# Which weight sums a transfer adds up, and when turned parts are copied out, in the MLP of a hybrid decoder block

## The chip, the core and the metric

The kernel runs on one core of a Trainium2 chip. Times are device microseconds for one execution. Its engines work side by side, each through its own list of instructions in order: PE (TensorE) multiplies, DVE (VectorE) and ACT (ScalarE) work on tiles elementwise, POOL (GpSimd) and SP (SyncE) here mostly issue transfers (DMAs). Engines wait for each other through semaphores.

## What is computed

One decoder layer for 256 tokens of width 2048 in float32: attention and a gated convolution, merged and added to the residual; an MLP; a gated per-layer embedding. The change lies in the MLP, the second line below:

```python
r = r + merged @ w_o[i]
h = rms_norm(r, g_mlp[i])
r = r + jnp.square(jax.nn.relu(h @ w_up[i])) @ w_down[i]   # w_up 2048 x 8192, w_down 8192 x 2048
h = rms_norm(r, g_ple[i])
r = r + jax.nn.sigmoid(h @ w_ple_gate[i]) * (p[i] @ w_ple_proj[i])
```

## The kernel before

**Splitting.** A float32 factor is multiplied as a high and a low part: ACT rounds the tile to `hi` (line 87, `w_hi`, `b_hi`, `t_hi`), DVE forms `lo` = tile − `hi` (line 101, `w_lo`, `b_lo`, `t_lo`), and PE (line 90) multiplies three of the four combinations.

**Units.** The MLP goes through 72 units `g`: 64 `up` units, each 128 columns of `w_up`, and 8 `dn` units, each 128 columns of the last quarter of `w_down`. PE does a unit's columns (`cols`, 32 matmuls into `ps_up` or `ps_dn`), then a piece of the product with the rest of `w_down`.

**Items.** That product uses a scheme of seven products per block of two by two, `P1` to `P7`, accumulated in seven PSUM banks over a run of items. An *item* (side, j) is one such block of weights; there are 56, numbered here from 0 in the order of `items`. Runs with one side follow each other: items 0 to 3, then five runs of eight (4 to 11, 12 to 19, ... 36 to 43), and a last one of twelve (44 to 55). Items 48 to 55 are *halved*: unit g = 55 makes the first half (0, 1) of item 48 and unit 56 the second half (2, 3), and so on to unit 70. The scheme needs sums of weight blocks. `load_pair` loads four blocks into `raw_s` (SP, 256 KB each), and `make` splits `B11` and `B22` (`b_hi`, `b_lo`), forms the sums for `T1`, `T3` (called `t13`) and later those for `T2`, `T4`, and splits these too (`t_hi`, `t_lo`). PE multiplies an item one unit after it was made.

**`ADDED`** (line 684) says for which items the two sums of `t13` are made by a transfer: `load_added` loads the third block twice into a tile `t` one unit ahead (SP), `load_pair` leaves that block out, and an accumulating DMA on POOL (line 702) adds two blocks of `raw_s` into `t`. For the other items DVE adds (`raw_s<-raw_s` 128x1024).

**Ends of runs.** At the end of a run the seven banks are copied by ACT (`part`) and added to DRAM by seven accumulating DMAs on POOL (`store`, line 825, `part_P<-part`). These are put into the list `filling`; `fill()` emits one at chosen places of the next unit's work.

**Parts into outputs.** Late in the MLP `fetch_part` loads the finished products (`part_in`, SP) for one side and half; `jobs` combine them (ACT scales, DVE `part_in<-part_in,scales`), up to four each time `run_jobs` is called, which only halved items do. Two results of each fetch are `turned`: `turn_part` transposes one on PE (line 863) into a bank of PSUM, ACT copies it out (`part_out`) and POOL adds it to the residual kept in DRAM (line 868, `r_kept`). The bank is the one that the next unit's columns write, so these wait for `part_out`. The transposes stand on PE between the first and the second piece of products of a halved unit. The copy goes through `filling` as well: in `make` it is emitted by a `fill()` behind the `high` of a sum.

The order of instructions on each engine is that of the code: every matmul, activation, DVE operation and SP load keeps its program order (`inorder`, `load`), and POOL's DMAs go out one after the other.

Of the kernel before, what the change touches and what calls it, by code (L numbers as in the profile page):

```python
# [38 lines left out]
def hybrid_block_kernel(ctx: ExitStack, tc: tile.TileContext, ins: dict, out: bass.AP):  # L39
# [571 lines left out]
    N_GROUP, GROUP = 6, 4  # L611
# [7 lines left out]
    NU = len(units)  # L619
# [4 lines left out]
    items = []  # L624
# [47 lines left out]
    def half_tiles(name):  # L672
        return tuple(wp.tile([P, HALF], F32R, tag=t, name=f"{name}_{t}") for t in ("hi", "lo"))
# [7 lines left out]
        wU[g].append((hi, lo))  # L681
        return lambda: high(hi, raw), lambda: low(lo, raw, hi)

    ADDED = set(items[4::2])

    def pair_part(a, n, d):
        side, j = a
# [16 lines left out]
    def load_added(a):  # L704

        wS[a] = {}
        if a in ADDED:
            t = wS[a]["t13"] = wp.tile([P, 2, CW], F32, tag="t", name="t13", bufs=2)
# [25 lines left out]
    def make(a, xs, evacuate, work):  # L734


        w, j = wS[a], a[1]
        raw = w["raw"]
        flat, halves = "p a f -> p (a f)", "p (a f) -> p a f"
        fresh = None  # L740
        if 0 in xs:
            if j not in sums:
                fresh = sum_u(j)
                sums[j] = tuple(slot([P, 4, P], F32R, f"s_{i}") for i in range(2))
            sh, sl = sums[j]
            for i in range(4):
                w[f"S{i + 1}"] = sh[:, i, :], sl[:, i, :]
            hi, lo = half_tiles("b")
            keep(w, ("B11", "B22"), hi, lo)
            src = raw[:, 0:2, :].rearrange(flat)  # L750
            high(hi, src)
            evacuate()
            if fresh is not None:
                high(sh, fresh)
            low(lo, src, hi)
            if a in ADDED:
                t13 = w["t13"]
            else:
                t13 = raw[:, 0:3:2, :]
                dve.tensor_add(t13, raw[:, 0:2, :], raw[:, 2:3, :].to_broadcast([P, 2, CW]))  # L760
            w["raw13"] = t13
        if 2 in xs:
            b21 = w["B21"] = tuple(slot([P, CW], F32R, f"b21_{n}") for n in range(2))
            high(b21[0], raw[:, 3, :])
            evacuate()
            fill()
            dve.tensor_add(raw[:, 1, :], raw[:, 1, :], w["raw13"][:, 0, :])
            if 0 in xs:
                low(b21[1], raw[:, 3, :], b21[0])
                dve.tensor_add(raw[:, 3, :], raw[:, 1, :], raw[:, 3, :])  # L770
                raw24 = raw[:, 1:4:2, :]
            else:
                dve.tensor_add(raw[:, 2, :], raw[:, 1, :], raw[:, 3, :])
                low(b21[1], raw[:, 3, :], b21[0])
                raw24 = raw[:, 1:3, :]
                work()
        if 0 in xs:
            if fresh is not None:
                low(sl, fresh, sh)
            if 2 not in xs:  # L780
                work()
            t13 = half_tiles("t13")
            keep(w, ("T1", "T3"), *t13)
            view = [t.rearrange(halves, a=2) for t in t13]
            high(view[0], w["raw13"])
            fill()
            low(view[1], w["raw13"], view[0])
        if 2 in xs:
            t24 = half_tiles("t24")
            keep(w, ("T2", "T4"), *t24)  # L790
            view = [t.rearrange(halves, a=2) for t in t24]
            high(view[0], raw24)
            fill()
            low(view[1], raw24, view[0])
# [36 lines left out]
    jobs, turns_due = [], []  # L831
# [27 lines left out]
    def turn_part(u, src):  # L859
        ps = bank("ps_part").rearrange("p (i s) -> p i s", i=2)  # L860
        for i in range(2):
            for t in range(NT):
                inorder(nc.tensor.transpose(ps[:, i, t * P:(t + 1) * P], src[t][:, i * P:(i + 1) * P], ident))

        def out():
            st = slot([P, 2, S], F32, "part_out")
            act(st, ps, AF.Copy)
            nc.gpsimd.dma_start(r_kept[u], st, accum_op=ALU.add)

        filling.append(out)  # L870

    filling = []

    def fill(n=1):
        for _ in range(min(n, len(filling))):
            filling.pop(0)()
# [61 lines left out]
        r[u] = slot([P, 2, S], F32, f"r_{u}")  # L938
        nc.gpsimd.dma_start(r[u], r_kept[u])

    fetching = {NU - 18: (1, 0), NU - 16: (1, 1), NU - 14: (0, 0), NU - 12: (0, 1)}

    for g in range(2):
        load_raw(g)
# [6 lines left out]
    for g in range(NU):  # L951
        kind, i = units[g]
        ordered[0] = g > 1
        if g in (5, 7):
            banks["acc"] = [7, 5] if g == 5 else [7]
        reach = 1 if FIRST <= g < NU - 8 else 2
        for n in range(g + 2, g + reach + 2):
            load_raw(n)
        for a, x in staged[g + 1]:
            if x == 0:  # L960
                load_pair(a)
        for a, x in staged[g + 2]:
            if x == 0:
                load_added(a)
        if g in fetching:
            fetch_part(*fetching[g])
        for u in {NU - 8: (4, 5, 6, 7), NU - 4: (0, 1), NU - 3: (2, 3)}.get(g, ()):
            load_r(u)
        if g == NU - 3:
            ss2 = slot([P, 2, S], F32, "ss2")  # L970
        if g == NU - 2:
            praw = slot([P, 2, S], F32, "p")
            load(praw, ins["pT"].rearrange("p (k s) -> p k s", s=S))
        xs = hT if kind == "up" else {k: uT[16 * i[0] + k] for k in range(16)}
        ps = cols(wU[g][1:], xs, f"{kind}_{g}")
        ending = any(a in last_of for a, _ in staged[g - 1])
        carried = len(filling)
        if ending:
            assert not filling
            for a, x in staged[g - 1]:  # L980
                products(a, x)
        if g == 0:
            rstd1 = rstd_columns(ss1, "mlp", 1)
            scales = const.tile([P, 2 * NT], F32, name="scales")
            dve.tensor_mul(scales[:, :NT], rstd1, rstd1)
            dve.tensor_scalar_mul(scales[:, NT:], scales[:, :NT], -1.0)
            up0, up1, down0, down1 = (scales[:, t:t + 1] for t in range(2 * NT))
        if g == 1:
            row1 = rstd_rows(rstd_diag(scales, "mlp"), "mlp")
        done = [n for n in range(g) if n in evac] if g > 1 else []  # L990
        ups = [units[n][1] for n in done if units[n][0] == "up"]
        for k in ups:
            up_sum(k, evac.pop(done.pop(0)))
        halves = []
        while made < g + reach:
            made += 1
            load_raw(made)
            halves += [(made, 0), (made, 1)]
        for h in halves:
            on_act, on_dve = unit_half(*h)  # L1000
            on_act()
            fill()
            on_dve()
        for k in ups:
            up_high(k)
        for k in ups:
            up_low(k)
        for n in done:
            dn_done(*units[n][1], evac.pop(n))
        taken = []  # L1010

        queue = [] if ending else list(staged[g - 1])

        def take():
            if taken:
                return
            taken.append(evacuated(ps, kind))
            if ending:
                side = staged[g - 1][0][0][0]
                filling.extend(lambda name=name: store(side, name) for name in NAMES)  # L1020
            if due and queue:
                products(*queue.pop(0))
                turn_part(*due.pop(0))

        due = [turns_due.pop(0)] if turns_due else []

        def run_jobs():
            for _ in range(min(4, len(jobs))):
                jobs.pop(0)()

        fill(carried)
        if staged[g]:
            make(staged[g][0][0], [x for _, x in staged[g]], take, run_jobs)
        take()
        if g == NU - 1:
            p1 = [evacuated(prod["P1"], "p1", by) for by in (up0, up1)]
            d, e = (slot([P, CW], F32, n) for n in "de")
            scaled(d, prod["P5"], up0, p1[0], ALU.subtract)
            scaled(e, prod["P3"], up0, d)
        entering = {NU - 2: (8, 9), NU - 1: (10, 11, 12, 13, 14)}.get(g, ())  # L1040
        for n in entering:
            enter_high(n)
            if n % 2 == 1:
                square(n // 2)
        for n in entering:
            enter_low(n)
        evac[g] = taken[0]
        if kind == "up" and i == 63:
            up_sum(i, evac.pop(g))
            up_high(i)  # L1050
            up_low(i)
        for a, x in queue:
            products(a, x)
        assert not due
# [188 lines left out]
```

## Time and profile before

| | us |
|---|---|
| median of 3 runs (lowest to highest) | 1442.47 (1440.68 to 1443.04) |
| the profiled execution | 1441.09 |
| its span | 1439.3 |
| PE busy in it | 1417.1 |

By stage, from the windows of the profile (length; busy time of PE, PEld, DVE, ACT and POOL with instructions; PE's clock as a share of full speed; mean DMA share; GB/s):

```profile
0.00:631.00 631.00, 629.52 (x2907) 523.29 (x2908) 404.93 (x680) 333.77 (x617) 139.93 (x230) 1.00 0.71 231
631.00:860.00 229.00, 229.00 (x1206) 197.42 (x1205) 201.67 (x282) 164.30 (x247) 15.87 (x24) 1.00 0.77 235
860.00:1170.00 310.00, 304.02 (x1541) 257.74 (x1541) 275.80 (x366) 224.15 (x328) 35.83 (x42) 0.99 0.91 255
1170.00:1284.00 114.00, 105.56 (x549) 88.58 (x548) 104.58 (x162) 80.17 (x122) 14.16 (x18) 0.97 0.93 269
1284.00:1334.00 50.00, 47.52 (x250) 40.19 (x250) 41.15 (x63) 27.75 (x39) 3.96 (x6) 0.99 0.70 216
1334.00:1439.30 105.30, 101.48 (x598) 89.77 (x596) 80.13 (x139) 55.49 (x95) 1.64 (x1) 0.99 0.41 145
```

All before the MLP lies ahead of 631 us. The MLP goes to about 1327; behind it come the gate of the embedding and the output. In every stage PE is busy for most of the time; where its busy time is short of the window, it waits. In rows of the timeline, `1.02 <-ACT up` in brackets at the end of a row says that the engine was idle for 1.02 us before it, and that ACT's instruction that wrote `up` ended that. Equal instructions that follow each other closely make one row (x2).

### The profile page before, as it was taken

The numbers are of one execution on the slowest core, as the hardware profiler recorded it, in microseconds if no ns is written. First come the engines' busy times: TensorE is split into PE (matmuls) and PEld (weight loads), VectorE is DVE, ScalarE is ACT, GpSimd is POOL, SyncE is SP. The second block draws the span as 40 slices with busy tenths as digits, with TensorE's granted clock in tenths as the row PEclk, the third lists the DMA queues.
The fourth block names the chain that finished last, engine by engine and source line by source line (L and its number), as shares of the span: only waits on it lengthen the run. The fifth ranks groups of instructions, "written<-read, shape, count | busy, mean of one in ns | idle before, by whom it ended". The sixth has DMA issues, their size and how long they took to land.

```text
span 1439.3 us, 19925 instructions
## 1 busy us (share of the span) xinstructions
PE 1417.1 (98%) x7041; PEld 1197.0 (83%) x7041; DVE 1108.2 (77%) x1688; ACT 885.6 (62%) x1446; POOL 211.4 (15%) x321
## 2 busy tenths in 40 slices
PE   9999999999999999999999999999999999989998
PEld 7888888888888888888888888887887877878888
DVE  7676666766565647757999989898979989978984
ACT  6765545554544544546777868676767867665752
POOL 0043464302020200000000101001010100110000
PEclk9999999999999999999999999999999999999999
DMA  9868787766666675645797978989898899996470
GB/s 279 307 224 250 228 248 238 234 208 208 209 207 204 215 256 205 212 165 172 222 299 237 312 232 240 267 238 274 246 254 248 243 296 264 262 276 208 144 259 23
DMA packets 224052, 335.07 MB, mean 233 GB/s; under 512 B 13904, under 2 KB 148304, under 8 KB 209872
## 3 DMA queue, kind: packets, MB, share of 16 engines
q1 hardware_dynamic: 204000, 287.61, 61.1%
q0 software_dynamic: 19808, 46.16, 14.2%
q8 instruction: 55, 0.90, 0.2%
q14 instruction: 45, 0.37, 0.1%
q10 hardware_dynamic: 144, 0.04, 0.0%
HBM read 294.95 MB, written 24.64 MB: 222 GB/s over the span
## 4 chain that ended last, share of the span: by engine, by line
PE 81%; DVE 8%; DMA 6%; issue 3%; ACT 2%; SPq 0%; DVEq 0%; POOLq 0%; ACTq 0%
PE ps_up L90 16%; PE ps_g L90 12%; PE P L90 11%; PE ps_o L90 7%; PE ps_pg L90 6%; PE ps_y L90 6%; DMA raw_s<-in_w_down_dram 4%; PE ps_q L90 3%; PE ps_k L90 3%; PE ps_cx L90 3%; PE ps_cb L90 3%; PE ps_cc L90 3%; PE ps_v L90 3%; PE ps_dn L90 3%; DMA t<-raw_s 2%
## 5 line engine op out<-in xcount | busy, mean ns | idle before, releaser
L101 DVE TENSOR_TENSOR w_lo<-raw,w_hi 128x512 fp32r<-128x512 f32 (+1 forms) x524 | 468.2, 927 | 186.6 <-ACT w_hi L87 161.0
L87 ACT ACTIVATE w_hi<-raw 128x512 fp32r<-128x512 f32 (+1 forms) x524 | 406.9, 816 | 259.3 <-PE ps_g L90 63.3
L90 PE MATMUL ps_up<-x,w_hi 128*128 128x512 f32 x1024 | 255.8, 393 | 6.5 <-ACT part_out L87 3.5
L90 PEld LDWEIGHTS ps_up<-x,w_hi 128*128 128x128 f32 x1024 | 192.4, 189 | 47.6 <-ACT up L87 5.9
L90 PE MATMUL ps_g<-w_hi,x 128*128 128x512 f32 x512 | 158.2, 389 | 0.0
L87 ACT ACTIVATE t_hi<-raw_s 128x1024 fp32r<-128x1024 f32 x86 | 91.2, 1061 | 84.7 <-DVE raw_s L101 84.7
L90 PEld LDWEIGHTS ps_up<-x,w_lo 128*128 128x128 f32 x1024 | 131.3, 191 | 5.0
L90 PE MATMUL ps_up<-x,w_lo 128*128 128x256 f32 x1024 | 132.8, 283 | 0.0
L90 PE MATMUL P<-t_hi,s 128*128 128x512 f32 x336 | 123.4, 394 | 0.3 <-ACT t_hi L87 0.3
L101 DVE TENSOR_TENSOR t_lo<-raw_s,t_hi 128x1024 fp32r<-128x1024 f32 x86 | 103.9, 1221 | 15.5 <-ACT t_hi L87 15.5
L90 PEld LDWEIGHTS ps_g<-w_hi,x 128*128 128x128 f32 x512 | 96.1, 188 | 19.9
L90 PE MATMUL ps_g<-w_lo,x 128*128 128x512 f32 x256 | 99.6, 389 | 0.0
L101 DVE TENSOR_TENSOR raw_s<-raw_s 128x512 f32<-128x512 f32 (+1 forms) x116 | 96.2, 829 | 3.8
L702 POOL DMA_DIRECT2D t<-raw_s x26 | 22.2, 853 | 447.7 <-DMA raw_s<-in_w_down_dram 199.5
L90 PE MATMUL ps_y<-w_hi,x 128*128 128x512 f32 x256 | 79.4, 389 | 0.0
L90 PEld LDWEIGHTS P<-t_hi,s 128*128 128x128 f32 x336 | 63.6, 189 | 13.2 <-ACT t_hi L87 0.7
L101 DVE TENSOR_TENSOR b_lo<-raw_s,b_hi 128x1024 fp32r<-128x1024 f32 x56 | 68.3, 1219 | 3.4 <-ACT b_hi L87 3.4
L90 PE MATMUL P<-t_lo,s 128*128 128x512 f32 x168 | 66.1, 394 | 3.7 <-DVE t_lo L101 3.7
L90 PE MATMUL ps_pg<-x,w_hi 128*128 128x512 f32 (+1 forms) x272 | 69.1, 385 | 0.5 <-DVE x L101 0.5
L87 ACT ACTIVATE up<-ps_up 128x512 f32<-128x512 f32 x64 | 37.6, 588 | 37.2 <-PE ps_up L90 37.2
L87 ACT ACTIVATE a<-a 128x256 f32<-128x256 f32 x128 | 53.2, 415 | 11.6 <-DVE a L101 9.6
L87 ACT ACTIVATE b_hi<-raw_s 128x1024 fp32r<-128x1024 f32 x56 | 58.8, 1050 | 1.8 <-PE ps_dn L90 1.8
(238 smaller groups left out, 2583.2 us busy)
## 6 DMA issues: line engine op xcount, KB each, us to landing
raw<-in_w_up_dram SPq DMA_DIRECT2D x64, 1024.0 KB, 7.6
raw<-in_w_in_dram SPq DMA_DIRECT2D x56, 1024.0 KB, 5.4
raw_s<-in_w_down_dram SPq DMA_DIRECT2D x198, 256.0 KB, 4.4
raw<-in_w_branch_dram SPq DMA_DIRECT2D x16, 1024.0 KB, 5.7
raw<-in_w_o_dram SPq DMA_DIRECT2D x16, 1024.0 KB, 4.9
t<-in_w_down_dram SPq DMA_DIRECT2D x52, 256.0 KB, 5.3
t<-raw_s POOLq DMA_DIRECT2D x26, 512.0 KB, 7.9
raw_first<-in_w_qkv_dram SPq DMA_DIRECT2D x48, 256.0 KB, 6.6
```

What stands on the lines that cost most here:

```text
L87: return inorder(nc.scalar.activation(*args, **kw))
L90: return inorder(nc.tensor.matmul(*args, **kw))
L101: return lambda *args, **kw: inorder(getattr(nc.vector, name)(*args, **kw))
L702: nc.gpsimd.dma_start(wS[a]["t13"], raw[:, 0:2, :], accum_op=ALU.add)
```

## The change

Three edits:
- `ADDED` held every second item from 4 on: in each run of eight the first, third, fifth and seventh, and in the last run 44, 46, 48, 50, 52, 54. It now holds the first, fifth and seventh of each run (44 of the last run's first four), and all of items 48 to 55. So items 6, 14, 22, 30, 38, 46 are added by DVE, and 49, 51, 53, 55 by transfer: 24 transfers instead of 26, of which 8 instead of 4 fall in the last run's halved items.
- The copy of a turned part goes into a list of its own, `turned_out`. `out_turned()` empties it in the second half of an item right behind the evacuation of the columns, in the first half ahead of `high` of the sum, and again behind `take()`.
- The four fetches move from g = 54, 56, 58, 60 to 53, 56, 59, 62; `run_jobs` does up to three jobs instead of four; a turn is taken from its list only in a unit with products to put it between.

```diff
-    ADDED = set(items[4::2])
+    LAST = len(items) - 8
+    ADDED = {items[n] for n in range(GROUP, LAST) if (n - GROUP) % (2 * GROUP) in (0, 4, 6)} | set(items[LAST:])
...
             high(b21[0], raw[:, 3, :])
             evacuate()
+            out_turned()
             fill()
...
             if 2 not in xs:
                 work()
+            out_turned()
             t13 = half_tiles("t13")
...
-        filling.append(out)
-
-    filling = []
+        turned_out.append(out)
+
+    filling, turned_out = [], []
+
+    def out_turned():
+        while turned_out:
+            turned_out.pop(0)()
...
-    fetching = {NU - 18: (1, 0), NU - 16: (1, 1), NU - 14: (0, 0), NU - 12: (0, 1)}
+    fetching = {53: (1, 0), 56: (1, 1), 59: (0, 0), 62: (0, 1)}
...
-        due = [turns_due.pop(0)] if turns_due else []
+        due = [turns_due.pop(0)] if turns_due and queue else []
 
         def run_jobs():
-            for _ in range(min(4, len(jobs))):
+            for _ in range(min(3, len(jobs))):
...
         take()
+        out_turned()
```

**ACT in units 57 and 58 (item 49).** Before: `b_hi` to `w_hi` is unit 57, the rest unit 58. `up` is the evacuation of the unit's columns, `s` and `part_in` are other work of the unit, `t_hi` the high part of a sum.

```order
L87 ACTIVATE b_hi<-raw_s 128x1024
L87 ACTIVATE up<-ps_up_11212 128x512
L87 ACTIVATE s_11265<-s_raw 128x512
L87 ACTIVATE part_in<-part_in,scales 128x256 x2
L87 ACTIVATE t_hi<-raw_s 128x1024
L87 ACTIVATE part_out<-ps_part 128x512
L87 ACTIVATE w_hi<-raw 128x1024 x2
L87 ACTIVATE a<-a 128x256 x2
L87 ACTIVATE x<-a 128x256
L87 ACTIVATE b_0_11369<-raw_s 128x512
L87 ACTIVATE up<-ps_up_11321 128x512
L87 ACTIVATE part_out<-ps_part 128x512
```

After, the same place:

```order
L87 ACTIVATE b_hi<-raw_s 128x1024
L87 ACTIVATE up<-ps_up_11201 128x512
L87 ACTIVATE s_11254<-s_raw 128x512
L87 ACTIVATE t_hi<-t_11009 128x1024
L87 ACTIVATE w_hi<-raw 128x1024 x2
L87 ACTIVATE a<-a 128x256 x2
L87 ACTIVATE x<-a 128x256
L87 ACTIVATE b_0_11336<-raw_s 128x512
L87 ACTIVATE up<-ps_up_11288 128x512
L87 ACTIVATE part_out<-ps_part 128x512
L87 ACTIVATE part_in<-part_in,scales 128x256 x2
L87 ACTIVATE t_hi<-raw_s 128x1024
```

The first turned part leaves unit 57 and comes out in unit 58, directly behind `up`; the sum of item 49 comes from `t` (a transfer) instead of `raw_s` (a sum by DVE).

**SP at units 53 and 54.** `t` and `raw_s` are the blocks of an item, `raw` the weights of a unit, `part_in` the fetch. Before:

```order
L96 DMA raw_s<-in_w_down_dram 128x4x128 x4
L96 DMA t_10819<-in_w_down_dram 128x4x128 x2
L96 DMA raw<-in_w_up_dram 128x2048
L96 DMA raw_s<-in_w_down_dram 128x4x128 x3
L96 DMA part_in<-part_P_5554 128x256
L96 DMA part_in<-part_P_5556 128x256
```

After:

```order
L96 DMA raw_s<-in_w_down_dram 128x4x128 x4
L96 DMA t_10806<-in_w_down_dram 128x4x128 x2
L96 DMA part_in<-part_P_5554 128x256
L96 DMA part_in<-part_P_5556 128x256
L96 DMA part_in<-part_P_5551 128x256
L96 DMA part_in<-part_P_5552 128x256
L96 DMA part_in<-part_P_5550 128x256
L96 DMA part_in<-part_P_5553 128x256
L96 DMA part_in<-part_P_5555 128x256
L96 DMA raw<-in_w_up_dram 128x2048
L96 DMA raw_s<-in_w_down_dram 128x4x128 x3
```

The seven loads of the fetch now stand ahead of the weights of unit 56 and of the blocks of item 48.

**POOL at the start of the last run.** `part_P` are the stores of the run that has ended, `t` the sums of items, `r_kept` the turned parts. Before:

```order
L825 DMA part_P_5555<-part 128x512
L702 DMA t_10595<-raw_s 128x1024
L825 DMA part_P_5556<-part 128x512
L702 DMA t_10819<-raw_s 128x1024
L702 DMA t_11209<-raw_s 128x1024
L868 DMA r_kept_4718<-part_out 128x512
L868 DMA r_kept_4720<-part_out 128x512
```

After:

```order
L828 DMA part_P_5555<-part 128x512
L828 DMA part_P_5556<-part 128x512
L703 DMA t_10806<-raw_s 128x1024
L703 DMA t_11009<-raw_s 128x1024
L703 DMA t_11198<-raw_s 128x1024
L871 DMA r_kept_4718<-part_out 128x512
L871 DMA r_kept_4720<-part_out 128x512
```

The sum of item 46 (`t_10595`) between the last two stores is gone, and the sum of item 49 (`t_11009`) has come in between those of items 48 and 50.

## The prediction

> **What bounds the kernel now.** I read the page's first part, then the windows of the MLP, where all edits lie, then PE's timeline there, and behind each of its gaps the timeline of the engine that ended it.
>
> ```profile
> PE 1417.1 (98%) x7041; PEld 1197.0 (83%) x7041; DVE 1108.2 (77%) x1688; ACT 885.6 (62%) x1446; POOL 211.4 (15%) x321
> 860.00:1284.00 424.00, 409.58 (x2089) 346.32 (x2089) 380.38 (x527) 304.32 (x448) 49.99 (x60) 0.99 0.92 259
> ```
>
> TensorE is the bound: the change leaves every matmul in place, so it can only win what PE loses. The second line is the window from 860 to 1284 us (length; busy time of PE, PEld, DVE, ACT, POOL; clock, DMA share, GB/s). PE idles 424.00 − 409.58 = 14.42 us there. These are PE's gaps of over 0.2 us in it (start, duration, what waited, in brackets the idle time and what ended it):
>
> ```profile
> 913.77 0.39 PE L90 MATMUL P<-t_hi,x 128*128 128x512 f32 x1
> 914.00 0.39 PE L90 MATMUL P<-t_lo,x 128*128 128x512 f32 x1
> ...
> 915.61 0.73 PE L90 MATMUL ps_up<-x,w_hi 128*128 128x512 f32 x2 [0.99 <-ACT up L87]
> 996.30 0.50 PE L90 MATMUL P<-t_lo,s 128*128 128x512 f32 x1 [0.66 <-DVE t_lo L101]
> 1000.79 0.73 PE L90 MATMUL ps_up<-x,w_hi 128*128 128x512 f32 x2 [1.02 <-ACT up L87]
> 1080.90 0.50 PE L90 MATMUL P<-t_hi,s 128*128 128x512 f32 x1 [0.29 <-ACT t_hi L87]
> 1083.05 0.50 PE L90 MATMUL P<-t_lo,s 128*128 128x512 f32 x1 [1.65 <-DVE t_lo L101]
> 1169.20 0.50 PE L90 MATMUL P<-t_lo,s 128*128 128x512 f32 x1 [1.36 <-DVE t_lo L101]
> 1173.69 0.50 PE L90 MATMUL ps_up<-x,w_hi 128*128 128x512 f32 x1 [1.02 <-ACT up L87]
> ...
> 1203.54 3.66 PE L90 MATMUL ps_up<-x,w_hi 128*128 128x512 f32 x9 [2.70 <-ACT part_out L87]
> 1222.82 0.50 PE L90 MATMUL ps_up<-x,w_hi 128*128 128x512 f32 x1 [0.81 <-ACT part_out L87]
> 1264.96 0.44 PE L863 MATMUL ps_part<-ident,part_in 128*128 128x128 f32 x2 [1.51 <-ACT dn L87]
> 1277.48 5.30 PE L90 MATMUL ps_dn<-x,w_hi 128*128 128x512 f32 x15 [2.40 <-ACT part_out L87]
> ```
>
> They come in two sorts. The seven up to 1174 recur every 85 to 86 us: the **middle**, once in each run of eight items. The other four lie in the **tail**, items 48 to 55.
>
> What a gap costs is more than its bracket. Matmuls start 0.23 us apart (913.77, 914.00) while each is shown 0.39 long, so a gap delays PE by its bracket plus 0.16. And behind the longest the clock is down:
>
> ```profile
> 1080.00:1090.00 10.00, 8.06 (x27) 5.93 (x26) 9.90 (x12) 7.31 (x11) 0.85 (x1) 0.83 0.86 281
> 1200.00:1210.00 10.00, 7.30 (x33) 5.86 (x32) 9.93 (x15) 6.18 (x11) 1.73 (x2) 0.83 0.96 245
> 1270.00:1280.00 10.00, 7.60 (x39) 6.17 (x38) 9.12 (x14) 6.18 (x9) 1.71 (x2) 0.90 1.09 320
> ...
> 1084.99 1.48 PE L90 MATMUL P<-b,x 128*128 128x512 f32 x3
> 1086.27 0.63 PE L90 MATMUL P<-t_hi,s 128*128 128x512 f32 x1
> ```
>
> Three matmuls from 1084.99 to 1086.27 are 0.43 us apart, 0.20 too much; the eight or so from 1083 on lose about 1.5 us. Nine at 1203.54 take 3.66 where 9 × 0.227 + 0.16 = 2.2, a loss of 1.4; fifteen at 1277.48 take 5.30 for 3.6, a loss of 1.7. So:
> - middle: brackets 6.99 + 7 × 0.16 + 1.5 = **9.6 us**
> - tail: brackets 7.42 + 4 × 0.16 + 3.1 = **11.2 us**
>
> By the Trainium skill ("TensorE: Matmul & The Clock Gate", Part 1) PE's clock halves only after an idle window of about 3.4 us. These gaps are 2.70 at most, so by it the slow matmuls have another cause and their 4.6 us would stay. The trace ties every slow stretch to a gap of 1.65 us or more and shows none without, so I count them as won; the other case is a rival below.
>
> **The change, part by part.**
>
> *The third of each run loses its transfer (six items).* What the gaps wait for, by the view of waits, the rows of one such item, and the table of transfers (median us to landing last):
>
> ```profile
> ACT t_hi L87 <- DMA t<-raw_s: 23.5, 4, 6.7
> DVE raw_s L101 <- DMA t<-raw_s: 17.2, 3, 6.5
> ...
> 899.90 0.85 POOL L702 DMA_DIRECT2D t<-raw_s  x1 [8.83 <-DVE w_lo L101]
> ...
> 900.81 1.22 DVE L101 TENSOR_TENSOR b_lo<-raw_s,b_hi 128x1024 fp32r<-128x1024 f32 x1
> 907.91 0.69 DVE L101 TENSOR_TENSOR raw_s<-raw_s,t 128x512 f32<-128x512 f32 x1 [5.88 <-DMA t<-raw_s]
> ...
> 907.86 1.06 ACT L87 ACTIVATE t_hi<-t 128x1024 fp32r<-128x1024 f32 x1 [6.08 <-DMA t<-raw_s]
> ...
> t<-raw_s POOLq DMA_DIRECT2D x26, 512.0 KB, 7.9
> part_P<-part POOLq DMA_DIRECT2D x42, 256.0 KB, 7.9
> ```
>
> ACT waits for an accumulating transfer four times, 23.5 us together, once in each of the last four long runs: this item follows the seven accumulating stores of the run before. Its sum is issued at 899.90 and lands 8 us later; DVE is free from 902.0, ACT from 901.8. PE's lead takes most of the 6 us and loses the rest. (In two earlier runs PE lost nothing, so nothing is won.) Afterwards one DVE add stands in place of the wait:
>
> ```profile
> L101 DVE TENSOR_TENSOR raw_s<-raw_s 128x1024 f32<-128x1024 f32 x30 | 36.8, 1225 | 1.0
> ```
>
> 1.2 us of DVE, from about 902.0, so `t_hi` can start near 903.3 instead of 907.9. These 4.6 us are more than the dearest of the four stalls cost PE (0.29 + 1.65 + 0.32 + 1.5 = 3.8, at 1083), so all **9.6 us** should go. What hides the add is DVE's room: a run occupies it for 78.3 us in 86.4 (the window below), with the add 79.5, while PE without its two gaps needs 86.4 − 2.4 − 0.3 = 83.7. That leaves 4 us; without them the adds would cost up to 1.2 us each, 5 in the four runs.
>
> ```profile
> 1087.60:1174.00 86.40, 84.02 (x428) 71.13 (x427) 78.29 (x105) 62.95 (x92) 9.43 (x11) 1.00 0.91 253
> ```
>
> What is late next is the third block of `raw_s`, which the add needs. The trace doesn't show it loaded for this item; the issue of the sum, which waits for its neighbours, bounds it at 899.9, and one more 256 KB load behind puts it near 901: just in time. POOL's seventh store moves ahead of where the sum stood and no longer waits for it.
>
> *All eight items of the last run get transfers (four new), and turned parts go out first.* A tail gap, as ACT and DVE show it:
>
> ```profile
> 1200.68 1.23 DVE L101 TENSOR_TENSOR raw_s<-raw_s 128x1024 f32<-128x1024 f32 x1
> ...
> 1201.94 1.06 ACT L87 ACTIVATE t_hi<-raw_s 128x1024 fp32r<-128x1024 f32 x1 [0.82 <-DVE raw_s L101]
> 1202.90 0.58 ACT L87 ACTIVATE part_out<-ps_part 128x512 f32<-128x512 f32 x1
> ...
> 1221.24 1.04 ACT L87 ACTIVATE t_hi<-t 128x1024 fp32r<-128x1024 f32 x1
> 1222.19 0.58 ACT L87 ACTIVATE part_out<-ps_part 128x512 f32<-128x512 f32 x1
> ...
> 1260.03 3.88 ACT L87 ACTIVATE w_hi<-raw 128x1024 fp32r<-128x1024 f32 x4
> ```
>
> PE's next columns write the bank that `part_out` empties. At 1202.90 it stands behind `t_hi`, and that behind the DVE add, while PE was through at 1203.54 − 2.70 = 1200.8. Ahead of `t_hi` it loses 0.82 + 1.06 us of delay, and the add that goes takes 1.23 off DVE: 3.1 against 2.70. (The first turned part moves to the next half, where its copy follows the evacuation `up` directly.) The gap of 0.81 behind 1222.19 is `t_hi` alone (1.04) and goes with the order. That of 2.40 (item 53) has the same chain as the first. That of 1.51 at 1264.96 is ACT behind four `w_hi`, which came late as DVE was behind; DVE is relieved of two adds ahead of it (items 49, 51), 2.45 us, which is more than 1.51. Sum **11.2 us**. If PE has not done the transposes when ACT arrives, ACT waits there instead; its cover is that it is busy only 54.6 of 81 us.
>
> The four new sums add, each, two loads less one and 512 KB of accumulation on POOL's queue, behind `r_kept`. Their cost is nothing if they land as the present ones do: `t_hi` at 1221.24 reads such a sum and has no bracket. At the other end a late sum costs PE what one costs in the middle, 1.2 us (915.61) to 3.8. I take 0, the row of the tail itself, and keep 3.8 for one of them, item 53, where DMA is at 1.09, for the range.
>
> *Fetching earlier, three jobs a time.* The jobs' cost stays and is spread. The first fetch moves one unit up, on SP ahead of the raw weights of unit 56:
>
> ```profile
> 1162.58 2.05 SPq L96 DMA_DIRECT2D raw<-in_w_up_dram  x1
> ...
> 1172.02 3.23 SPq L96 DMA_DIRECT2D part_in<-part_P  x7
> ```
>
> Behind seven loads, 3.2 us, that load comes at worst 3.2 us later, with `w_hi`, the columns and PE behind it; at best no later, as two `t` loads and the 512 KB of a dropped sum no longer stand ahead of it. I take 1 us.
>
> **Sum.** 1441.09 (the profiled run, whose span is 1439.3) − 9.6 − 11.2 + 1 = 1421.3. The three runs' median, 1442.47, lies 1.4 higher, so I say **1422**.
>
> **The rivals.**
> - *Tail waits are replaced.* ACT now waits at `part_out` for PE, or the sums land late; PE keeps its 11.2: 1431.5. For it: DMA share 0.96 to 1.09 there. Against: `t_hi` at 1221.24. 0.13.
> - *Middle wait is replaced.* The fourth `raw_s` load lands as late as the sum did; 9.6 stays: 1431. For it: the 8 us that the stores take to land. Against: it needs one landing fewer. 0.07.
> - *The slow clock is not of the gaps' making.* Its 4.6 us stay: 1426. It is the rule named above. 0.05.
> - *The change does not reach PE.* Emptied ahead, `part_out` still ends where PE waits, and the middle's adds wait for late loads: both halves are replaced, within 0.2% of 1442.5. 0.06.
> - *Slower: the last run's sums land behind `r_kept`.* ACT's `t_hi` then blocks `w_hi` and the evacuations behind it on ACT. Beyond 20.8 / 4 = 5.2 us lost to PE per new sum it turns slower; a wait as in the middle, 6 us, with no lead of PE to take it gives 4 × 6 − 20.8: 1445. Against it: no sum of the tail shows a wait now. 0.07.
> - The forecast, all but a little won: 1418 to 1426. 0.62.
>
> **How the numbers follow.** A measurement of this kernel can tell about 0.2% (2.9 us). Faster 0.62 + 0.13 + 0.07 + 0.05 = 0.87, same 0.06, slower 0.07. The range runs from 1418, with nothing given back and the lower of the two times before, to 1433, the two half gains with a little given back; what lies above is 0.13, and the rest of the 2 in 10 lies at its edges.
>
> **What would show it.** Right: no row `t_hi <- DMA t<-raw_s` of 23 us in the waits; no bracket over 0.3 on PE from 860 to 1284, PE's idle time there under 3 us, the clock at 1.00; `part_out` ahead of `t_hi` and ended before PE's columns. Wrong: `t_hi` waiting for `t<-raw_s` in the tail; `w_hi` waiting for raw weights at unit 56; a DVE without idle time that ends PE's gaps; gaps of PE of the same sum elsewhere, above all past 1284, where the last parts wait for ACT and DVE and where a shift could cost what was won.

## The result, and the profile after

| | before | after |
|---|---|---|
| median (lowest to highest), us | 1442.76 (1440.68 to 1445.99), 4 runs | 1432.58 (1430.71 to 1433.82), 4 runs |
| ratio, 95% interval | | 0.9926 [0.9905, 0.9948] |
| profiled execution, its span, us | 1441.09, 1439.3 | 1432.14, 1430.3 |

The changed kernel is 10.2 us (0.7%) faster: just inside the upper edge of the range (1433), and half of the 20.5 us forecast (1442.47 to 1422). The windows of the changed kernel (length; busy time of PE, PEld, DVE, ACT, POOL; clock; DMA share; GB/s) tell where the other half is missing:

```profile
860.00:1170.00 310.00, 310.00 (x1596) 266.18 (x1595) 296.42 (x390) 237.15 (x345) 33.36 (x39) 1.00 0.92 259
1170.00:1284.00 114.00, 104.05 (x553) 88.32 (x551) 91.54 (x149) 72.32 (x108) 14.79 (x20) 0.97 0.94 264
```

In the middle PE loses nothing any more: it is busy 310.00 of 310.00 us, where it was 304.02. The tail is worse: 104.05 of 114, where it was 105.56. From 1170 to 1290 the timeline of PE shows three gaps instead of four:

```profile
1239.31 0.79 PE L90 MATMUL ps_up<-x,w_hi 128*128 128x512 f32 x1 [8.28 <-ACT part_out L87]
1257.32 0.44 PE L866 MATMUL ps_part<-ident,part_in 128*128 128x128 f32 x2 [1.52 <-ACT dn L87]
1285.24 0.50 PE L90 MATMUL ps_dn<-x,w_hi 128*128 128x512 f32 x1 [1.39 <-ACT part_out L87]
```

One gap of 8.28 us is new. It is at the fourth turned part, in unit 62. What ACT did there, from its timeline, and what POOL did, from its own:

```profile
1221.59 0.58 ACT L87 ACTIVATE part_out<-ps_part 128x512 f32<-128x512 f32 x1
...
1238.66 0.60 ACT L87 ACTIVATE part_out<-ps_part 128x512 f32<-128x512 f32 x1 [9.97 <-DMA r_kept<-part_out]
...
1227.42 0.85 POOL L703 DMA_DIRECT2D t<-raw_s  x1 [15.65 <-DMA part_in<-part_P]
1227.96 1.19 POOL L871 DMA_DIRECT2D r_kept<-part_out  x1
```

Read from the bottom up. The third turned part was copied out at 1221.59 to 1222.17, but its transfer to DRAM was issued only at 1227.96: it stood on POOL behind the sum of item 52 (1227.42), which belongs to unit 62 and waited for loads. In the code the sum comes second: unlike what is said ahead of the prediction, POOL's transfers need not go out in the order of the code. The transfer landed 10.6 us after its issue, near 1238.6. The fourth copy, at 1238.66, waited 9.97 us for that landing, though it reads something else: it is written to the buffer that the third copy still held. PE's next columns wait for the fourth copy. All tiles of the kind `slot` (`part_out`, `x`, `b`, `s`, `part_in` and others) share 44 buffers (`N_SLOT`); a new tile takes a buffer whose last reader may still be a transfer under way. The addresses in the program as built (they are no view of the profile) say the same: the fourth copy lies where the third lay, and `x` of the next unit where the fourth lay.

### The profile page after: what moved, and what is told of

Read it like the earlier page. It is cut to its first block, busy times and chain, and to the rows that moved or that the text cites. A ratio compares the mean times of both kernels' runs of the same rounds, so it can differ in the third digit from the quotient of the medians.

```text
span 1430.3 us, 19936 instructions
## 1 busy us (share of the span) xinstructions
PE 1411.4 (99%) x7041; PEld 1196.5 (84%) x7041; DVE 1110.8 (78%) x1690; ACT 886.8 (62%) x1446; POOL 208.5 (15%) x319
## 4 chain that ended last, share of the span: by engine, by line
PE 95%; DMA 2%; DVE 1%; ACT 1%; issue 0%; SPq 0%; POOL 0%; DVEq 0%; POOLq 0%; ACTq 0%
PE ps_up L90 25%; PE P L90 18%; PE ps_g L90 12%; PE ps_o L90 7%; PE ps_pg L90 6%; PE ps_y L90 6%; PE ps_q L90 3%; PE ps_k L90 3%; PE ps_cx L90 3%; PE ps_cb L90 3%; PE ps_cc L90 3%; PE ps_v L90 3%; PE ps_dn L90 2%; PE ps_proj L90 1%; DMA r_kept<-part_out 1%; DMA t<-raw_s 1%
## 5 line engine op out<-in xcount | busy, mean ns | idle before, releaser
L101 DVE TENSOR_TENSOR raw_s<-raw_s 128x512 f32<-128x512 f32 (+1 forms) x120 | 100.1, 834 | 4.1
L703 POOL DMA_DIRECT2D t<-raw_s x24 | 20.5, 854 | 461.1 <-DMA raw_s<-in_w_down_dram 119.6
```

What stands on the lines that cost most here:

```text
L101: return lambda *args, **kw: inorder(getattr(nc.vector, name)(*args, **kw))
L703: nc.gpsimd.dma_start(wS[a]["t13"], raw[:, 0:2, :], accum_op=ALU.add)
```

## The experiments

Two questions: is the gap of 8.28 us really made by the buffer and POOL's order, and what is each edit worth alone? "Before" in this section is the kernel before, run beside each experiment (medians 1442.3 to 1443.2).

**e1: POOL in the order of the code.** On the changed kernel:

```diff
-            nc.gpsimd.dma_start(r_kept[u], st, accum_op=ALU.add)
+            tc.keep_in_program_order(nc.gpsimd.dma_start(r_kept[u], st, accum_op=ALU.add))
...
-            nc.gpsimd.dma_start(wS[a]["t13"], raw[:, 0:2, :], accum_op=ALU.add)
+            dma = nc.gpsimd.dma_start(wS[a]["t13"], raw[:, 0:2, :], accum_op=ALU.add)
+            if a[1] >= N_BOTH:
+                tc.keep_in_program_order(dma)
```

> The changed kernel, with the transfers of turned parts and the sums of items from 48 on issued by POOL in the order of the code, which moves one row: the third turned part's `r_kept<-part_out` goes ahead of the sum of item 52 instead of behind it. Theory (the fourth `part_out` waits for its buffer, which the third one holds until its transfer lands, and that transfer stood on POOL behind a sum that waits for loads): the transfer is issued near 1222.3 instead of 1227.96 and lands 6.3 to 6.9 us later as the two before it do, by 1229, before PE has done the transposes (1229.9); the gap of 8.3 us at 1239 goes, with 1.6 us of slow matmuls behind it: about 10 us faster than the changed kernel, 1422 to 1423. Rival (the transfer lands late since the DMA engines are crowded there, not since it is issued late): it lands at 1232 or later, a gap of 2 us or more stays, 1425 to 1432.

Measured: 1426.18 us, ratio to before 0.9885 [0.9872, 0.9899], 6 us faster than the changed kernel. POOL, ACT and PE of this kernel:

```profile
1222.53 0.85 POOL L873 DMA_DIRECT2D r_kept<-part_out  x1 [10.22 <-ACT part_out L87]
...
1230.88 0.85 POOL L873 DMA_DIRECT2D r_kept<-part_out  x1 [2.61 <-ACT part_out L87]
...
1240.12 0.42 ACT L87 ACTIVATE x<-a 128x256 fp32r<-128x256 f32 x1 [5.80 <-DMA r_kept<-part_out]
...
1242.02 3.72 PE L90 MATMUL ps_dn<-x,w_hi 128*128 128x512 f32 x15 [3.04 <-ACT up L87]
```

The third transfer goes out at 1222.53 as expected, lands 6.8 us later, at 1229.3, and the fourth copy no longer waits. But now `x` waits 5.80 us for the *fourth* transfer (issued 1230.88, landed 9.2 us later, by 1240.1): it is the next tile to take that buffer. The gap shrinks from 8.28 to 3.04 us and moves one unit on. The theory of the order holds for the third transfer; the expected 1422 to 1423 does not, and time and remaining gap are those of the rival.

**e2: copied into the tile that was read.** On the changed kernel, `turn_part` gets the `part_in` tile `st` whose two parts it transposes, and copies into it:

```diff
-    def turn_part(u, src):
+    def turn_part(u, src, st):
...
-            st = slot([P, 2, S], F32, "part_out")
             act(st, ps, AF.Copy)
```

> The changed kernel, with a turned part copied by ACT into the tile that the transposes have read, instead of into a fresh slot; POOL's order stays, so the third transfer is late as before. Theory (it is the buffer that ACT waits for): ACT's copy waits for PE alone, the gap at 1239 goes though the third transfer still lands near 1238: about 1422 to 1423. Rival (ACT waits there for the late transfer for another reason, or the sum of item 52 comes late for itself): the wait moves to `t_hi` of item 52 or to the copy behind, and 3 to 8 us stay, 1425 to 1432.

Measured: 1429.56 us, 0.9908 [0.9893, 0.9923]. The copy waits for PE alone, as expected, and DVE waits instead. The expected 1422 to 1423 fell:

```profile
1236.30 0.69 DVE L101 TENSOR_TENSOR b<-raw_s,b 128x512 fp32r<-128x512 f32 x1 [7.17 <-DMA r_kept<-part_in]
```

**e5: one buffer more.** On the changed kernel; the instructions of ACT, DVE, PE and SP stay in the same order:

```diff
-N_SLOT = 44
+N_SLOT = 45
...
-        return sm.tile([P, S], F32, tag="temp", name=name, bufs=10)
+        return sm.tile([P, S], F32, tag="temp", name=name, bufs=8)
```

> The changed kernel with 45 tiles instead of 44 in the pool that `part_out`, `x`, `b`, `s` and `part_in` share (room taken from two of the ten `temp` tiles); each engine's instructions stay in the same order. Theory (the gap of 8.3 us, and those that took its place in the two runs before, are tiles of this pool that wait for the buffer of a turned part until its transfer has landed): with one tile more the copy takes another buffer, ACT and DVE wait for no `r_kept` in units 61 to 63, the gap goes without a new one in its place, the gaps of 1.5 at 1257 and 1.4 at 1285 stay: 1420 to 1423. Rival (crowded transfers make something late there anyway): 3 us or more of gaps stay in those units, 1425 or more.

Measured: 1430.16 us, 0.9912 [0.9899, 0.9925]. The expectation fell, and its row says how:

```profile
1237.48 0.69 DVE L101 TENSOR_TENSOR b<-raw_s,b 128x512 fp32r<-128x512 f32 x1 [9.22 <-DMA r_kept<-part_out]
```

With one more buffer the tiles fall on other buffers: the copy is free, and `b` of the same unit, which in the program as built has the third copy's buffer, waits 9.22 us. PE has four gaps of 1.1 to 2.1 us from 1238 to 1255 instead of the one of 8.28 and that of 1.52. So e1, e2 and e5 agree on the mechanism (a tile of the pool waits for a turned part's transfer) and show that it is not one unlucky tile: whichever takes the buffer next waits, as long as the transfers land late, here 8.8 to 10.6 us after their issue.

**e3: the middle alone.** On the kernel before:

```diff
-    ADDED = set(items[4::2])
+    LAST = len(items) - 8
+    ADDED = {items[n] for n in range(GROUP, LAST) if (n - GROUP) % (2 * GROUP) in (0, 4, 6)} | set(items[LAST::2])
```

> The kernel before, with only the third of each run taken out of the transfers (items 6, 14, ... 46 by DVE); last run, order and fetches as before. Theory (the middle's seven gaps cost 9.6 us and all of it is won by this): 9 to 11 us faster than before, 1432 to 1434, no wait of ACT for `t<-raw_s`, the four gaps of the tail as before. Rival (part of what the changed kernel won in the middle comes from the other edits, as the earlier fetch): under 7 us, 1436 or more.

Measured: 1426.52 us, 0.9889 [0.9875, 0.9902]: 16.1 us faster than before, where 9 to 11 were expected, and 6 us faster than the whole change. PE's gaps in its tail:

```profile
1191.58 0.50 PE L90 MATMUL ps_up<-x,w_hi 128*128 128x512 f32 x1 [0.83 <-ACT part_out L87]
1209.51 0.50 PE L90 MATMUL ps_up<-x,w_hi 128*128 128x512 f32 x1 [0.81 <-ACT part_out L87]
1251.69 0.33 PE L864 MATMUL ps_part<-ident,part_in 128*128 128x128 f32 x1 [1.51 <-ACT dn L87]
1264.20 5.17 PE L90 MATMUL ps_dn<-x,w_hi 128*128 128x512 f32 x15 [2.40 <-ACT part_out L87]
```

They are the four gaps of before, at the same instructions, and three have their old lengths (0.81, 1.51, 2.40). The first, 2.70 before, is 0.83 here, though nothing in the tail was changed. The time came out below the expected 1432 to 1434.

**e4: the tail alone.** On the changed kernel:

```diff
-    ADDED = {items[n] for n in range(GROUP, LAST) if (n - GROUP) % (2 * GROUP) in (0, 4, 6)} | set(items[LAST:])
+    ADDED = set(items[4:LAST:2]) | set(items[LAST:])
```

> The changed kernel, with the sums of items 4 to 46 by transfer as before (every second): the edits of the last run alone, but for the fetch, which moves too. Theory (the tail lost 11.2 us before and loses 13 to 14 after, as one gap of 8.3 took the place of the others): 1443 to 1446, 1 to 3 us slower than before, with the seven gaps of the middle as before and the gap behind `part_out` in unit 62. Rival (the tail's edits win by themselves): 1440 or less.

Measured: 1453.42 us, 1.0072 [1.006, 1.0085]: 10.8 us *slower* than before, where 1 to 3 were expected. Besides the gap in unit 62 (5.60 here) there is a new one of 9.33 us at 1172. Its row on PE, ACT's wait, and POOL:

```profile
1172.34 1.22 PE L90 MATMUL ps_up<-x,w_hi 128*128 128x512 f32 x2 [9.33 <-ACT up L87]
...
1170.44 0.42 ACT L87 ACTIVATE x<-a 128x256 fp32r<-128x256 f32 x1 [10.66 <-DMA part_P<-part]
...
1160.50 0.88 POOL L703 DMA_DIRECT2D t<-raw_s  x1 [9.86 <-DMA raw_s<-in_w_down_dram]
1161.05 1.22 POOL L828 DMA_DIRECT2D part_P<-part  x1
```

It is the same mechanism at another place: with the fetch one unit earlier, `x` takes the buffer of the run's seventh `part`, whose store stands on POOL behind the sum of item 46. In the whole change that sum is gone, and so is this gap. So what an edit is worth depends on the others.

**e6 to e11: each edit on the middle.** All have the middle of e3; they add the order of the copies (O: `turned_out`), the eight sums (S: `set(items[LAST:])`) and the fetches with three jobs (F), alone or in pairs. In e6 and e9 the fetches are put back:

```diff
-    fetching = {53: (1, 0), 56: (1, 1), 59: (0, 0), 62: (0, 1)}
+    fetching = {NU - 18: (1, 0), NU - 16: (1, 1), NU - 14: (0, 0), NU - 12: (0, 1)}
...
-            for _ in range(min(3, len(jobs))):
+            for _ in range(min(4, len(jobs))):
```

in e6 and e10 the sums (`set(items[LAST::2])`), in e11 the order (`filling.append(out)` for `turned_out.append(out)`); e7 and e8 put back the two that they lack. The third edit's condition on turns (`and queue`) stays in all of them and is no part of F.

> The kernel before with the third of each run taken out, as in e3, and the turned parts copied out ahead of the high part; last run's sums and fetches as before. Theory (in e3 three of the four gaps left, lost 1.0, 1.0 and 2.6 us, are `part_out` behind `t_hi`): these go or shrink by 1 us each, 1422 to 1425. Rival (the new order is what made the tail worse): 1428 or more.

> As e3, with all eight sums of the last run by transfer; copies and fetches as before. Theory (four more sums relieve DVE by 1.2 us each and land in time, and `part_out` still stands behind `t_hi`): the gap of 2.6 falls to about 1, 1424 to 1426.5. Rival (the sums land late, or put the turned parts' transfers late on POOL, and block ACT): 1429 or more.

> As e3, with the fetches at 53, 56, 59, 62 and three jobs a time; sums and copies as before. Theory (it takes the three edits together to make a tile wait for a buffer: the fetches hold tiles longer, the sums put the transfer late on POOL): no gap over 3 us, 1425 to 1429. Rival (the fetches alone make it): a gap of 5 us or more behind a tile that waits for `r_kept`, 1431 or more.

> The changed kernel with the fetches and jobs as before: the middle, the order and the eight sums. Theory (the sums' own price in e7 is item 53: its sum lands late and `part_out` stands behind the `t_hi` that waits for it; ahead of `t_hi` the copy is free of that): the gap of 5.1 us at 1267 falls under 2, 1420 to 1424. Rival (the late sum also holds the `w_hi` and evacuations behind it on ACT, whatever the order): 3 us or more stay, 1425 or more.

> The changed kernel with the sums of the last run as before (48, 50, 52, 54): the middle, the order and the fetches. Theory (the fetches make a turned part's copy wait for the buffer of the one before it, 3.7 us of ACT in e8; it does so in this order too): a gap of 1 to 4 us behind the fourth `part_out`, 1421 to 1426. Rivals: with the copies ahead the buffer is free in time, no gap over 1 us but the one at unit 64, 1420 or less; or the copies come closer to each other and wait longer, a gap over 5 us, 1428 or more.

> The changed kernel with the copies of turned parts behind the high part, as before: the middle, the sums and the fetches. Theory (the gap of 8.3 comes of sums and fetches together; the order only takes the copies from behind `t_hi`, which won 6.7 us in e6 against e3): the wait for the buffer stays at 8 us or more of ACT, 1436 to 1441. Rival (the order itself brings the fourth copy too early for its buffer): 1434 or less.

Measured, medians in us (ratio to before, interval):

| on the middle | copies behind `t_hi` | copies ahead (O) | O wins |
|---|---|---|---|
| nothing | e3 1426.52 | e6 **1419.83** (0.984 [0.9827, 0.9853]) | 6.7 |
| S | e7 1433.96 (0.9936 [0.9921, 0.995]) | e9 1424.28 (0.9884 [0.9867, 0.9901]) | 9.7 |
| F | e8 1429.93 (0.9908 [0.9893, 0.9923]) | e10 1426.61 (0.9888 [0.9875, 0.9902]) | 3.3 |
| S and F | e11 1437.24 (0.9968 [0.9956, 0.9981]) | the whole change 1432.58 | 4.7 |

The runs of one kernel scatter by up to 7.3 us here: e8's six lie from 1425.25 to 1432.59, and e7's in two groups, two near 1430 (the profiled one is of these) and four from 1433.8 to 1435.3. So differences of 3 us between two medians are rough.

*The order is the good edit of the tail.* It wins in each row. In e6, where 1422 to 1425 were expected, it leaves one gap in the tail:

```profile
1248.01 0.44 PE L866 MATMUL ps_part<-ident,part_in 128*128 128x128 f32 x2 [1.68 <-ACT dn L87]
...
1170.00:1284.00 114.00, 112.32 (x607) 96.07 (x606) 104.88 (x162) 80.45 (x118) 17.29 (x23) 1.00 0.96 280
```

*The sums cost 4.5 to 7.4 us* (e9 − e6, e7 − e3; with F 6.0 and 7.3), where e7 was expected to gain by them. In e7, POOL, ACT and PE at item 53, one of the four new sums:

```profile
1254.98 0.87 POOL L703 DMA_DIRECT2D t<-raw_s  x1 [0.39 <-DVE b L101]
...
1265.59 1.06 ACT L87 ACTIVATE t_hi<-t 128x1024 fp32r<-128x1024 f32 x1 [4.35 <-DMA t<-raw_s]
1266.55 0.58 ACT L87 ACTIVATE part_out<-ps_part 128x512 f32<-128x512 f32 x1
...
1267.19 0.79 PE L90 MATMUL ps_dn<-x,w_hi 128*128 128x512 f32 x1 [4.94 <-ACT part_out L87]
```

The sum lands 10.5 us after its issue, `t_hi` waits 4.35 us for it, and `part_out` behind it makes PE's gap 4.94 instead of 2.40. (This execution is 4.1 us faster than e7's median; no trace shows what its slower runs lose beside this.) In e9, with the copy ahead, `t_hi` still waits 3.50 us at the same item, and PE has no gap there, as expected. But e9 has waits of the other kind, by its view of waits (us in total, times, longest):

```profile
ACT up L87 <- DMA r_kept<-part_out: 7.1, 2, 3.6
```

Here it is `up`, the evacuation itself, that twice waits for a buffer of a turned part, and PE's two gaps in those units are 2.05 and 0.91 us. So the sums cost in two ways, by coming late themselves and by waits for the turned parts' transfers. (The profiled execution of e9 was the longest of its five, 1430.61, and has a gap of 3.34 us at 1318 where the other kernels have 0.5; how large its waits are at the median of 1424.28, no trace shows.)

*The fetches cost 3.3 to 8.3 us* (e8 − e3, e10 − e6; with S 3.3 and 8.3), and they make the wait for the buffer, with the old sums as well. The fourth `part_out` on ACT in e8, e10 and e11, one row each:

```profile
1234.00 0.60 ACT L87 ACTIVATE part_out<-ps_part 128x512 f32<-128x512 f32 x1 [3.69 <-DMA r_kept<-part_out]
```

```profile
1235.96 0.60 ACT L87 ACTIVATE part_out<-ps_part 128x512 f32<-128x512 f32 x1 [6.47 <-DMA r_kept<-part_out]
```

```profile
1240.91 0.60 ACT L87 ACTIVATE part_out<-ps_part 128x512 f32<-128x512 f32 x1 [8.95 <-DMA r_kept<-part_out]
```

In e8 and e10 the third turned part's transfer is issued behind the sum of item 52 on POOL too. e11 keeps the wait at 8.95 us without the order, so the order does not make it. Its time lies in the 1436 to 1441 expected; e10's gap of 4.78 us and its time lie a little above the 1 to 4 us and 1421 to 1426 expected. What I expected of e8 ("it takes the three edits together") fell in its mechanism, though its time was near: the fetches are enough for a wait of 3.7 us, the sums lengthen it. e3 and e6, without fetches and sums, have no row of ACT or DVE that waits for `r_kept`; e12 below, without them too, has one of 1.4 us (`up`). The programs as built show what the fetches do: in the whole change, e1, e4, e8, e10 and e11 the fourth copy has the third's buffer, in the six kernels with the old fetches (before, e3, e6, e7, e9 and e12) it has another, and the buffers of the first and the fourth copy go to `up` of units 59 and 61, which are the two that wait in e9.

**e12: four halves split in two goes.** On e6:

```diff
+        late = halves[2:] if g == NU - 8 else []
-        for h in halves:
+        for h in halves[:len(halves) - len(late)]:
...
+        for h in late:
+            for part in unit_half(*h):
+                part()
         take()
         out_turned()
```

> As e6 (the middle and the order, without sums and fetches), and in unit 64, where four halves of weights are split instead of two, two of them only behind the item's work, so that the evacuation of the columns stands behind two `w_hi` on ACT instead of four. Theory (the gap of 1.7 us at 1248 in e6 is that evacuation): it goes, 1417.5 to 1419. Rival (what is split later is late for the item or the next unit): 1420 or more.

Measured: 1421.12 us, 0.9848 [0.9835, 0.9862], not faster than e6, as its rival had it. The gap of 1.68 at 1248 is gone, and one of 1.38 behind `part_out` has come one unit later:

```profile
1260.08 0.50 PE L90 MATMUL ps_dn<-x,w_hi 128*128 128x512 f32 x1 [1.38 <-ACT part_out L87]
```

The best version is **e6: 1419.83 us**, 23 us faster than before and 12.7 faster than the change: the middle's half of the first edit and the order, without the eight sums and the third edit.

## Why the prediction came out as it did

- *The bound, and what a gap costs.* The bound is right. The rival on the clock (its 4.6 us stay) is out: in e6, where all gaps but one of 1.68 are gone, the clock is 1.00 in the tail. The trace agrees with the Trainium skill ("TensorE: Matmul & The Clock Gate", Part 1) in that the clock goes down behind an idle time and not otherwise, but not in the size: e3's gap of 2.40 us, shorter than 3.4, has 5.17 us for the fifteen matmuls behind it, where 3.6 is normal. Nor does the length of a gap settle it. A gap of e7 and, again, that of e1:

```profile
1208.61 5.30 PE L90 MATMUL ps_up<-x,w_hi 128*128 128x512 f32 x15 [1.80 <-ACT part_out L87]
...
1242.02 3.72 PE L90 MATMUL ps_dn<-x,w_hi 128*128 128x512 f32 x15 [3.04 <-ACT up L87]
```

The shorter gap has slow matmuls behind it, the longer has none. So the 4.6 us are what one execution lost, and no fixed price of these gaps.
- *The middle, 9.6 us.* Right in mechanism, too small. PE idles nowhere from 860 to 1170, and the add costs nothing that can be seen: DVE has 296.42 of 310 us to do and PE is never short. e3 won 16.1, 6.5 more than the term. Half of that is a cut by place: the first gap of the tail, 2.70 with slow matmuls behind it, is the aftermath of item 46. ACT and DVE wait near 1166 for its sum, and DVE comes late to the add at 1200.68: in the kernel before it is busy without a break up to there, in the window from 1174 to 1203 for 28.76 of 29.00 us (third number):

```profile
1174.00:1203.00 29.00, 26.84 (x142) 22.58 (x140) 28.76 (x46) 21.63 (x34) 0.85 (x1) 1.00 1.01 312
```

In e3 DVE has room ahead of the same gap (21.22 of 24.00 us from 1167 to 1191), and the gap is 0.83 with no slow matmuls: 3.3 us of what I booked under the tail. What follows from a place's wait was booked under the place where it came out. In the profiled executions e3 wins 14.2 us (1441.09 to 1426.87), of which 9.6 and 3.3 make 12.9; 1.3 stay open, and the other 1.9 of the 16.1 are the distance of these two executions from their medians.
- *The tail, 11.2 us.* Half right. "Turned parts go out first" did what was said: 6.7 us in e6 against e3, where the three gaps behind `part_out` are gone. With the middle it makes 1419.8, 2 us less than I had forecast for the whole (1422). The gap of 1.51 did not go: it is 1.52 in the changed kernel, though the adds of items 49 and 51 are off DVE. So DVE was at most a small part of its cause; it went only in e12, where ACT evacuates behind two `w_hi` instead of four.
- *"Their cost is nothing if they land as the present ones do"* (the four new sums). This step failed. I had taken one row of the tail, `t_hi` at 1221.24, for all, and named item 53 as the risk with 3.8 us; there the sum lands 10.5 us after its issue, and the sums cost 4.5 us or more, part of it by waits for buffers (e9). That they relieve DVE won little: the gap of 1.51 is 1.22 in e7 and 1.52 in the changed kernel.
- *"I take 1 us" for the earlier fetches.* This step failed by most: 8.3 us beside the other edits. The cost that I worked out, late raw weights of unit 56, did not occur: the changed kernel has no gap there. What I did not look at is the pool of buffers. The fetches move when tiles are held, so that copies and `x` take buffers whose transfers are still under way.
- *The rivals.* "Tail waits are replaced", 1431.5 with a chance of 0.13, gave the time (by the sum's own terms it is 1421.3 + 11.2 = 1432.5; the forecast likewise, 1421.3 + 1.4, is 1422.7 rather than 1422), and its row (ACT at `part_out`) is the one that waits; but ACT waits neither for PE nor for a sum, it waits for a buffer. The slower rival did not come for the whole change; e4 shows that without the middle's edit the rest is slower by 10.8 us.

So the sum, from runs: −16.1 (the middle) − 6.7 (the order) + 4.5 (the sums) + 8.3 (the fetches) = −10.0, against the measured −10.2. It is one way through the table, from e3 by e6 and e9 to the whole change, and adds up by construction; by another way the sums and the fetches have other prices. That the measured time lies in the range is partly luck: what the middle won beyond its term paid for half of what the sums and the fetches cost. Not settled: how the sums' cost divides between their own lateness and the buffers, and whether it is the earlier fetches or the three jobs a time that make the buffers short; they were not parted.

## What to carry to other kernels

A wait on a transfer in a profile may be a wait for a *buffer*: look whether the waiting instruction reads what the transfer wrote or writes over what it still reads. Before moving loads or copies in a kernel with a shared pool, ask which tile each moved one now follows in the pool, and which queue frees that buffer. When stalls follow each other, undo the first one alone and look at the rest before pricing them: here the first took with it 3.3 us that had been booked under the others.

## What the hardware showed beside this

The same transfer of 256 KB takes very different times. The table of transfers of the changed kernel, for what was issued at 1227.96 and at 1197.39 (KB each, us to landing):

```profile
r_kept<-part_out POOLq DMA_DIRECT2D x1, 256.0 KB, 10.6
...
r_kept<-part_out POOLq DMA_DIRECT2D x1, 256.0 KB, 6.9
```

The one of 10.6 us was issued half a microsecond behind a sum of 512 KB. Thirteen such transfers, one or two in nearly every run here, went out within 0.6 us behind a sum, and took 7.1 to 11.0 us. Some others took as long (9.1 us in e6, 23 us behind the last sum), so the sum is not the only cause, and which of them makes the other late was not tried; a plan that counts on the median of 4.9 us for it, as the table of the kernel before has it, is 5.7 us short there.
